# The second FFN's output pass in rows: activations held in TensorE, weights streamed, and the residual turned during the input pass

## Chip, cores and metric

One core of one Trainium2 chip. The metric is the device time of the program in microseconds (us); the kernel before takes 1973.4 us, the median of 3 runs (1972.02 to 1973.48).

## What is computed

One layer of a decoder on 1024 tokens of width 1024 in float32: an FFN of half weight, a mixing part (a gated recurrence and an attention, side by side), and a second FFN of half weight. Only the second FFN matters here:

```python
def swiglu(h, w_in, w_out):
    gu = h @ w_in
    g, u = jnp.split(gu, 2, axis=-1)
    return (jax.nn.silu(g) * u) @ w_out
...
        h = h + 0.5 * swiglu(rms_norm(h, ffn2_norm[l]), ffn2_w_in[l], ffn2_w_out[l])
    return h[:, pad + N_META:, :]
```

`w_in` is 1024 x 5632, `w_out` 2816 x 1024. The output is (1, 1024, 1024): tokens by features, so a row of the output is a token.

## The kernel before

Inside the kernel the residual h lies turned: `hT[:, m, t]` holds feature 128 m + p of token t on partition p. After the mixing part its turned form is also in DRAM, as `h2D` (8 blocks of 128 features x 1024 tokens), because the second FFN normalizes the copy on chip in place.

Both passes of the FFN use a fast (Strassen-Winograd) form of a 2 x 2 block product: seven block products in place of eight. Every float32 operand is split into a rounded part and the rest ("wh" and "wl" for a weight, "xh" and "xl" for an activation), and each product is three matmuls: wh by xh, wl by xh, wh by xl.

*Input pass* (`fast_in`, line 359). Columns of `w_in` are taken 128 at a time, in pairs f, f+1; a pair has two quads: the first (the "gate" quad, line 537) applies SiLU, the second (the "up" quad, line 546) multiplies. One quad loads four blocks of 128 x 4 x 128 from `w_in` (`block`, line 376, on SP's queue, each bound behind the one before), makes four sums of them on GpSimd (`made`, line 385), splits seven operands (`operand`, line 367: ScalarE rounds at L369, VectorE subtracts at L371), and runs seven products of 12 matmuls each (`times`, L458) into the banks qa, qb and qc, two buffers each. VectorE adds bank and kept parts (L490, L541, L548, L551, L552). The activations go to DRAM (`actD`) by GpSimd's queue, and some of their sums too (`combined`, line 562). The first four quads use weights split earlier; 18 quads follow that load from `w_in`.

*Output pass* (`fast_out`, line 624). `w_out` is taken as 2 x 2 blocks of 1408 x 512, and the activations as 2 x 2 blocks of 1408 features x 512 tokens. Seven steps (A12, A11, S1, S2, S4, S3, A22, line 709) each go over q = 0..10; a q loads a weight block and an activation block of 128 x 512 on SP's queue, splits both (`halved`, line 652, ScalarE L656 and VectorE L657, four places each in `parts`, so up to four q ahead), and runs 12 matmuls (L733): four blocks m of 128, three products each. The stationary operand is a 128 x 128 block of the weight, the moving one the activations of 512 tokens, so bank m gets 128 features x 512 tokens. Bank sets x and y are used in turn; x is started in A11 and added to in S2, S3 and A22, y is started in A12 and S1 and added to in S4. `evict` (line 700) adds half a bank to the residual on VectorE (L703): of A12, A11, S1, S2 and S4 in the next step, at q = 1 and q = 3; of S3 and A22 at once. The quadrants are final after A11, S4, S3 and A22.

The residual is loaded from `h2D` into `hT` on SP's queue during A12, A11 and S2 (line 2347). When the second half of the tokens is final (after S3) and when the first is (after A22), `store_out` (line 1058) turns it back: for four blocks of 128 tokens and two halves of the features, four TensorE transposes (L1065) into a bank, a copy by ScalarE (L1068) or VectorE (L1070), and a store of 256 KB on SP's queue (L1071).

TensorE runs in the order of the code; the other engines' orders come from a scheduler, which `issue_after` binds. An engine's queue runs in order, so a DMA that waits on SP holds all that is behind it.

The first FFN does a like turning of its input x during its own input pass (`turn_x`, line 1016): load, a VectorE transpose of 32 x 32 blocks (L1047), and four stores of 64 KB each in pieces of 32 elements (L1050).

Of the kernel before, what the change touches and what calls it, by code (L numbers as in the profile page):

```python
# [11 lines left out]
F32 = mybir.dt.float32  # L12
# [8 lines left out]
P = 128  # L21
# [28 lines left out]
class Block:  # L50
# [308 lines left out]
    def fast_in(self, ops, n, w_in, actD, openers, ev0, open_ev, feed=None, meta=None, spare=None,  # L359
# [7 lines left out]
        def operand(src):  # L367
            hi = wp.tile([P, 4, P], F32R, tag="wh", name="wh", bufs=3)
            nc.scalar.copy(hi, src)  # L369
            lo = wp.tile([P, 4, P], F32R, tag="wl", name="wl", bufs=3)  # L370
            nc.vector.tensor_sub(lo, src, hi.bitcast(F32))  # L371
            return hi, lo

        loaded, put_off, last_kept = [], [], []
# [1 line left out]
        def block(i, h, col):  # L376
            t = wp.tile([P, 4, P], F32, tag="raw", name="raw", bufs=self.in_bufs)
            with self.tc.issue_after(loaded[-1].ins) if loaded else ExitStack():
                loaded.append(nc.sync.dma_start(
                    t, w_in[512 * h : 512 * h + 512, col + P * i : col + P * i + P]  # L380
                    .rearrange("(k p) f -> p k f", p=P)
                ))
            return t

        def made(x, op, y, turns):
# [236 lines left out]
            put_off.pop()()  # L622

    def fast_out(self, hT, cs, n, w_out, actD, ready, between=lambda a, q: None,
                 meta=lambda a, q, blocks: None):

        nc = self.nc
        op, ring, pout = self.op, self.ring, self.pout
# [70 lines left out]

        def evict(bank, i, j, step, ms=range(4)):  # L700
            for m in ms:
                h = hT[:, 4 * i + m, cs[j] : cs[j] + n]
                nc.vector.scalar_tensor_tensor(  # L703
                    h, banks[bank][m], 0.5, h, ALU.mult, ALU.add
                )
            if 3 in ms:
                ready(step)

# [6 lines left out]
        for bank, a, b, start, (i, j) in steps:  # L715
            if start:
                banks[bank] = [
                    pout.tile([P, n], F32, tag=f"{bank}{m}", name="o") for m in range(4)
                ]
            for q in range(nq):  # L720
                with self.tc.issue_after(los[-4]) if self.apart and len(los) > 4 else ExitStack():
                    src, blocks = left(a, q)
                act = right((q, b), n)
                with self.tc.high_priority() if self.apart and a == "A12" and q < 3 else ExitStack():
                    wh, wl = halved(src, "w", 512)
                    xh, xl = halved(act, "t", n)
                order = [(m, e, q, wh, wl, xh, xl) for m in range(4) for e in range(3)]
                if a == "A12" and q < 3:
                    opening += order
                    order = sorted(opening, key=lambda o: (o[1], o[2])) if q == 2 else []  # L730
                for m, e, at, wh, wl, xh, xl in order:
                    y, z = ((wh, xh), (wl, xh), (wh, xl))[e]
                    nc.tensor.matmul(  # L733
                        banks[bank][m], y[:, m * P : (m + 1) * P], z,
                        start=start and at == 0 and e == 0,
                        stop=q == nq - 1 and e == 2, skip_group_check=True,
                    )
                meta(a, q, blocks)
                between(a, q)
                if q in (1, 3) and delayed:  # L740
                    evict(*delayed[0], range(q - 1, q + 1))
                    if q == 3:
                        delayed.pop()
            if a in ("S3", "A22"):
                evict(bank, i, j, a)
            else:
                delayed.append((bank, i, j, a))
# [307 lines left out]
                row = load(i + 1)  # L1055
            yield

    def store_out(self, hT, pool, pps, c0, n, tag):
        nc = self.nc
        for i, r0 in enumerate(range(c0, c0 + n, P)):  # L1060
            for q in range(2):
                row = pool.tile([P, 512], F32, tag="orow", name="orow", bufs=4)
                ps = pps.tile([P, 4, P], F32, tag=f"{tag}{(2 * i + q) % 4}", name="o")
                for k in range(4):
                    nc.tensor.transpose(ps[:, k, :], hT[:, 4 * q + k, r0 : r0 + P], self.ident)  # L1065
                dst = row.rearrange("p (k c) -> p k c", k=4)
                if q == 0:
                    nc.scalar.copy(dst, ps)  # L1068
                else:
                    nc.vector.tensor_copy(dst, ps)  # L1070
                nc.sync.dma_start(self.out[0, r0 : r0 + P, 512 * q : 512 * q + 512], row)  # L1071

    def proj_bank(self, n):
        self.proj_tags.reverse()
# [686 lines left out]
    def run(self):  # L1761
# [21 lines left out]
        with ExitStack() as c0:  # L1783
            with ExitStack() as c1:
# [373 lines left out]
                with tc.manual_schedule(engines={nc.tensor.engine}):  # L2158
# [38 lines left out]

                    self.weave(rest(), heads[:3], 1e6, 1.0, True)
            self.h2D = self.dram.tile([KT, P, SEQ], F32, name="h2D")
            ph = self.pool("h2")  # L2200
            hT = ph.tile([P, KT, SEQ], F32, tag="h2", name="hT2", bufs=1)
            (cA, n), (cB, _) = ((0, 512), (512, 512))
# [10 lines left out]
            with tc.manual_schedule(engines={nc.tensor.engine}), ExitStack() as cx:  # L2213
# [94 lines left out]
                rs = []  # L2308
                made = feed()
                def after_opened():  # L2310
                    both = ph.tile([P, 16, n], F32R, tag="h2", name="parts", bufs=1)
                    self.parts = {"w": both[:, :8], "t": both[:, 8:]}

                steps = self.fast_in(
                    ops, n, a["ffn2_w_in"][0], actD, 2, ev0, open_ev, made,
                    after_opened=after_opened,
                )
                next(steps)
                r = self.inv_rms_rows(sums[1], n, px, ppb)
# [6 lines left out]
                drain(steps)  # L2326
            with tc.manual_schedule(engines={nc.tensor.engine}), ExitStack() as c1:
                self.ring = self.pool("ring", ctx=c1, side="right")
                hT = self.pool("h3", ctx=c1).tile([P, KT, SEQ], F32, name="hT3")
                self.op = self.pool("op", ctx=c1)  # L2330
                self.pout = self.pool("pout2", 1, PSUM, c1)
                fin = self.pool("fin", ctx=c1)

                def ready(step):
                    if step == "S3":
                        self.store_out(hT, fin, self.pout, cB, n, "y")
                    elif step == "A22":
                        self.store_out(hT, fin, self.pout, cA, n, "y")

                loads = {("A12", 2 * m): (m, cA) for m in range(4)}  # L2340
                loads.update({("A11", m): ((m + 4) % 8, cB) for m in range(8)})
                loads.update({("S2", m): (m + 4, cA) for m in range(4)})

                def between(step, q):
                    if (step, q) in loads:
                        m, c = loads[step, q]
                        nc.sync.dma_start(hT[:, m, c : c + n], self.h2D[m, :, c : c + n])

                self.ring_bufs, self.act_bufs, self.apart = 6, 6, False
                self.fast_out(hT, (cA, cB), n, a["ffn2_w_out"][0], actD, ready, between)  # L2350


NAMES = [
# [21 lines left out]
```

## Time and profile before

| | |
|---|---|
| median of 3 runs | 1973.4 us |
| profiled execution | 1973.63 us |
| its span in the profile | 1971.9 us |
| granted clock of TensorE, mean | 0.999 |
| TensorE matmul busy | 1936.1 us (98%) |
| VectorE, ScalarE, GpSimd busy | 1390.4, 854.9, 445.0 us |
| output pass of the second FFN, start to last matmul | 1748.92 to 1962.36 us |

Positions are microseconds from the span's start. PE is TensorE's matmuls, PEld its weight loads (they overlap), DVE VectorE, ACT ScalarE, POOL GpSimd, SP SyncE; a q behind the name means the engine's queue, with its DMA issues and waits. A row of the timeline gives start, length, engine, line, operation, tile written <- tiles read, shapes, count, and in brackets the idle time of the engine before it and what ended it.

### The profile page before, as it was taken

To read this page: it belongs to the slowest core of one execution; us is meant where nothing else is said; L and a number is where in the kernel's file an instruction comes from. 1 tells how busy PE (TensorE), PEld (TensorE's weight loads), DVE (VectorE), ACT (ScalarE), POOL (GpSimd) and SP (SyncE) were. 2 spreads that over 40 slices of the span, in tenths; PEclk is the share of its full clock that TensorE was granted. 3 is DMA by queue.
4 is the path that set the end of the run, shared out by engine and by line. 5 is a ranking of instruction groups with operands and counts; after the bars stand their busy time and mean duration, and the time that the engine had idled before them with its cause. 6 is when DMAs were issued, how large, how long until landed. Compare 5 with 4: busy or idle time off the path is not lost.

```text
span 1971.9 us, 30437 instructions
## 1 busy us (share of the span) xinstructions
PE 1936.1 (98%) x10768; PEld 1629.3 (83%) x10768; DVE 1390.4 (71%) x2178; ACT 854.9 (43%) x1719; POOL 445.0 (23%) x614
## 2 busy tenths in 40 slices
PE   7999999999999999999999999999999999999998
PEld 6888888888888888888898978887888888888887
DVE  7977777877678665467777666667577766767764
ACT  6523343334444544366666635433223333344443
POOL 3010100001000003133333342210545544620000
PEclk9999999999999999999999999999999999999999
DMA  7356787758966325765454178646433323378463
GB/s 210 93 164 169 250 272 240 243 192 299 371 217 189 117 61 149 178 181 146 126 148 118 58 248 244 161 184 203 160 106 108 108 94 104 102 281 295 123 193 139
DMA packets 346362, 347.17 MB, mean 176 GB/s; under 512 B 94993, under 2 KB 250513, under 8 KB 346209
## 3 DMA queue, kind: packets, MB, share of 16 engines
q1 hardware_dynamic: 325360, 283.73, 47.1%
q0 software_dynamic: 19808, 61.49, 9.0%
q8 instruction: 85, 1.39, 0.3%
q14 instruction: 69, 0.56, 0.1%
q10 hardware_dynamic: 1040, 0.00, 0.0%
HBM read 233.75 MB, written 111.38 MB: 175 GB/s over the span
## 4 chain that ended last, share of the span: by engine, by line
PE 73%; issue 16%; DVE 4%; DMA 2%; POOL 2%; ACT 2%; SPq 1%; POOLq 0%; DVEq 0%; ACTq 0%
PE o L733 21%; PE qb L458 11%; PE qa L458 8%; PE qc L458 7%; PE proj L258 4%; PE proj L260 4%; PE proj L259 4%; PE flip L1479 2%; PE wo L259 1%; PE wo L258 1%; PE wo L260 1%; PE oacc L1554 1%; PE oacc L1556 1%; PE z L1624 1%; DMA KB<-hg_k 1%
## 5 line engine op out<-in xcount | busy, mean ns | idle before, releaser
L458 PE MATMUL qb<-T,wh 128*128 128x512 f32 x1056 | 344.4, 390 | 1.3 <-ACT T L318 0.8
L458 PEld LDWEIGHTS qb<-T,wh 128*128 128x128 f32 x1056 | 198.1, 188 | 46.1 <-issue 2.5
L458 PE MATMUL qa<-B,wh 128*128 128x512 f32 x696 | 226.8, 391 | 0.0
L258 PE MATMUL proj<-xh,wh 128*128 128x512 f32 (+2 forms) x640 | 213.4, 333 | 2.4 <-ACT st L1126 1.3
L733 PE MATMUL o<-t,w 128*128 128x512 f32 x924 | 212.2, 390 | 0.6 <-DVE u L551 0.5
L260 PE MATMUL proj<-xl,wh 128*128 128x512 f32 (+2 forms) x640 | 209.8, 328 | 0.8 <-DVE xl L1948 0.8
L733 PE MATMUL o<-parts 128*128 128x512 f32 x924 | 209.9, 389 | 0.0
L259 PE MATMUL proj<-xh,wl 128*128 128x512 f32 (+2 forms) x640 | 209.8, 328 | 0.0
L458 PE MATMUL qb<-T,wl 128*128 128x512 f32 x528 | 205.5, 389 | 0.0
L733 PEld LDWEIGHTS o<-t,w 128*128 128x128 f32 x924 | 172.7, 188 | 37.8 <-issue 0.8
L733 PEld LDWEIGHTS o<-parts 128*128 128x128 f32 x924 | 173.3, 188 | 36.0
L371 DVE TENSOR_TENSOR wl<-s,wh 128x512 fp32r<-128x512 f32 x160 | 165.7, 1035 | 50.8 <-ACT wh L369 49.8
L369 ACT CAST wh<-s 128x512 fp32r<-128x512 f32 x160 | 99.4, 622 | 194.1 <-PE qb L458 146.1
L458 PEld LDWEIGHTS qa<-B,wh 128*128 128x128 f32 x696 | 130.7, 188 | 27.3 <-DVE B L837 0.3
L369 ACT CAST wh<-raw 128x512 fp32r<-128x512 f32 x120 | 74.4, 621 | 148.0 <-PE qc L458 108.0
L458 PE MATMUL qa<-B,wl 128*128 128x512 f32 x348 | 135.6, 390 | 0.0
L258 PEld LDWEIGHTS proj<-xh,wh 128*128 128x128 f32 x640 | 120.6, 188 | 14.4 <-ACT st L1126 1.9
L260 PEld LDWEIGHTS proj<-xl,wh 128*128 128x128 f32 x640 | 120.4, 188 | 12.1 <-DVE xl L1948 1.2
L259 PEld LDWEIGHTS proj<-xh,wl 128*128 128x128 f32 x640 | 120.5, 188 | 9.9
L458 PE MATMUL qc<-T,wh 128*128 128x512 f32 x352 | 117.1, 394 | 0.0
L458 PE MATMUL qc<-B,wh 128*128 128x512 f32 x352 | 115.0, 390 | 1.4 <-DVE u L551 1.4
L458 PEld LDWEIGHTS qb<-T,wl 128*128 128x128 f32 x528 | 99.1, 188 | 20.3
(399 smaller groups left out, 3865.6 us busy)
## 6 DMA issues: line engine op xcount, KB each, us to landing
raw<-in_ffn_w_in_dram SPq DMA_DIRECT2D x176, 256.0 KB, 4.1
raw<-in_ffn_w_out_dram SPq DMA_DIRECT2D x112, 256.0 KB, 4.3
w2in<-both SPq DMA_DIRECT2D x28, 512.0 KB, 3.4
raw<-in_w_in_dram SPq DMA_DIRECT2D x25, 512.0 KB, 5.2
ks<-kD SPq DMA_DIRECT2D x32, 260.0 KB, 4.8
wout<-both SPq DMA_DIRECT2D x16, 512.0 KB, 3.8
wh<-w2in SPq DMA_DIRECT2D x27, 256.0 KB, 3.3
wl<-w2in SPq DMA_DIRECT2D x27, 256.0 KB, 3.2
```

Of the source, the lines that this page charges most:

```text
L258: nc.tensor.matmul(ps, wh[:, s], xs, start=k == 0, stop=False)
L259: nc.tensor.matmul(ps, wl[:, s], xs, start=False, stop=False)
L260: nc.tensor.matmul(ps, wh[:, s], xl[:, k, c0 : c0 + n], start=False, stop=k == nk - 1)
L369: nc.scalar.copy(hi, src)
L371: nc.vector.tensor_sub(lo, src, hi.bitcast(F32))
L458: nc.tensor.matmul(ps, a[:, k, :], b[:, k, :], start=start and k == 0 and i == 0, stop=k == 3 and i == 2, skip_group_check=True,)
L733: nc.tensor.matmul(banks[bank][m], y[:, m * P : (m + 1) * P], z, start=start and at == 0 and e == 0, stop=q == nq - 1 and e == 2, skip_gro ...
L1479: self.nc.tensor.transpose(ps[:m, j, :], src[:, s0 : s0 + m], self.ident)
L1554: nc.tensor.matmul(o[:, c], vj, w[0], start=j == 0, stop=False, skip_group_check=True)
L1556: nc.tensor.matmul(o[:64, c], vj[:, :64], w[1], start=False, stop=end, skip_group_check=True)
L1624: nc.tensor.matmul(z, q, ks[0][:, s0 : s0 + n], start=True, stop=False)
```

## The change

1. In the output pass of the second FFN the two operands of each matmul change places (`rows=True`): the stationary block is 128 tokens of the activation, the moving one 512 features of the weight. Bank m then holds 128 tokens x 512 features, and the residual tile is `hR`, with rows of tokens.
2. The final quadrants are stored from `hR` straight after their eviction, 128 tokens x 512 features at a time: those of A11, S4 and S3 on GpSimd's queue, those of A22 on SP's. `store_out`, its TensorE transposes and its copies are gone.
3. The residual must be there in rows. A new generator, `turn_back`, goes over 16 places (8 blocks of features x 2 halves of the tokens) during the input pass, a step after each of the 18 quads: it loads 128 x 512 of `h2D`, transposes 32 x 32 blocks on VectorE (bound behind the last "wl" of the quad), and stores it in four pieces into `h2R` in DRAM (bound behind the quad's last weight load). The output pass loads `hR` from `h2R`, in the places where it loaded `hT` from `h2D`.

```diff
@@ operand, block (fast_in)
-            nc.vector.tensor_sub(lo, src, hi.bitcast(F32))
+            self.block_lo = nc.vector.tensor_sub(lo, src, hi.bitcast(F32))
...
+            self.block_load = loaded[-1]
@@ evict (fast_out)
-                h = hT[:, 4 * i + m, cs[j] : cs[j] + n]
+                h = (hT[:, 4 * j + m, 512 * i : 512 * i + 512] if rows
+                     else hT[:, 4 * i + m, cs[j] : cs[j] + n])
                 nc.vector.scalar_tensor_tensor(
                     h, banks[bank][m], 0.5, h, ALU.mult, ALU.add
                 )
+                if rows and step in ("A11", "S4", "S3", "A22"):
+                    r0 = n * j + P * m
+                    eng = nc.sync if step == "A22" else nc.gpsimd
+                    eng.dma_start(self.out[0, r0 : r0 + P, 512 * i : 512 * i + 512], h)
...
                     y, z = ((wh, xh), (wl, xh), (wh, xl))[e]
+                    if rows:
+                        y, z = z, y
                     nc.tensor.matmul(
                         banks[bank][m], y[:, m * P : (m + 1) * P], z,
@@ store_out is replaced by
+    def turn_back(self, pool, src, dst):
+        nc, tc = self.nc, self.tc
+        places = [(m, half) for half in range(2) for m in range(KT)]
+        def load(i):
+            m, half = places[i]
+            t = pool.tile([P, 512], F32, tag="hcol", name="hcol", bufs=2)
+            with tc.issue_after(self.block_load.ins):
+                nc.sync.dma_start(t, src[m, :, 512 * half : 512 * half + 512])
+            return t
+        def store(t, m, half):
+            for b in range(4):
+                c0 = P * m + 32 * b
+                with tc.issue_after(self.block_load.ins):
+                    nc.sync.dma_start(
+                        dst[512 * half : 512 * half + 512, c0 : c0 + 32]
+                        .rearrange("(f j) d -> j f d", j=32),
+                        t[32 * b : 32 * b + 32].rearrange("j (f d) -> j f d", d=32),
+                    )
+        cols = load(0)
+        yield
+        for i, place in enumerate(places):
+            t = pool.tile([P, 512], F32, tag="hrow", name="hrow", bufs=2)
+            with tc.issue_after(self.block_lo.ins):
+                nc.vector.transpose(t, cols)
+            if i + 1 < len(places):
+                cols = load(i + 1)
+            yield
+            store(t, *place)
@@ run
+                    back.append(self.turn_back(self.pool("hturn", ctx=cx), self.h2D, h2R))
...
-                    after_opened=after_opened,
+                    after_opened=after_opened, between=turn_next,
...
-                hT = self.pool("h3", ctx=c1).tile([P, KT, SEQ], F32, name="hT3")
+                hR = self.pool("h3", ctx=c1).tile([P, SEQ // P, D], F32, name="hR")
...
-                        nc.sync.dma_start(hT[:, m, c : c + n], self.h2D[m, :, c : c + n])
+                        r, i = loads[step, q]
+                        nc.sync.dma_start(
+                            hR[:, r, 512 * i : 512 * i + 512],
+                            h2R[P * r : P * r + P, 512 * i : 512 * i + 512],
+                        )
```

How it moves instructions shows at three places. On TensorE, from the end of the input pass to the end of the program, before ("qc" is the input pass, "o<-parts" the output pass, "o<-ident" the transposes):

```order
L458 MATMUL qc<-B_14181,wl 128x512
L458 MATMUL qc<-B_14182,wh 128x512
L733 MATMUL o<-parts 128x512 x792
L1065 MATMUL o<-ident,hT_17639 128x128 x32
L733 MATMUL o<-parts 128x512 x132
L1065 MATMUL o<-ident,hT_17639 128x128 x32
```

and now:

```order
L459 MATMUL qc<-B_14183,wh 128x512
L459 MATMUL qc<-B_14182,wh 128x512
L459 MATMUL qc<-B_14182,wl 128x512
L459 MATMUL qc<-B_14183,wh 128x512
L741 MATMUL o<-parts 128x512 x924
```

The two runs of 32 transposes are gone, and the 924 matmuls of the output pass follow each other.

On VectorE, in a gate quad of the input pass, where its last operand is split, before ("wl" is the rest of a split weight, "sg" and "u" are sums of banks):

```order
L371 TENSOR_TENSOR wl<-raw,wh 128x512
L490 TENSOR_TENSOR u_15238<-qb,p_15177 128x512
L371 TENSOR_TENSOR wl<-s,wh 128x512
L541 TENSOR_TENSOR sg<-qc,u_15238 128x512
L371 TENSOR_TENSOR wl<-raw,wh 128x512
L541 TENSOR_TENSOR sg<-qb,p_15177 128x512
L371 TENSOR_TENSOR wl<-s,wh 128x512
```

and now:

```order
L371 TENSOR_TENSOR wl<-raw,wh 128x512
L491 TENSOR_TENSOR u_15248<-qb,p_15187 128x512
L371 TENSOR_TENSOR wl<-s,wh 128x512
L1092 STREAM_TRANSPOSE hrow<-hcol 128x512
L542 TENSOR_TENSOR sg<-qc,u_15248 128x512
L371 TENSOR_TENSOR wl<-raw,wh 128x512
L542 TENSOR_TENSOR sg<-qb,p_15187 128x512
L371 TENSOR_TENSOR wl<-s,wh 128x512
```

The transpose stands between the split of the quad's last operand and the sum of bank qc; in an up quad it stands in front of the sum of L551 in the same way.

On SP's queue, over the 18 quads, before (72 weight loads in one row, then the output pass begins):

```order
L402 DMA wl<-w2in_908 128x512
L402 DMA wh<-w2in_908 128x512
L379 DMA raw<-in_ffn_w_in_dram 128x4x128 x72
L642 DMA raw<-in_ffn_w_out_dram 128x512
L647 DMA act<-act0B_12583 128x512
```

and now, at the start of the 18 quads ("hcol" is the loaded piece, "hrow" the transposed one; the last three rows go on alike for the other places):

```order
L1074 DMA hcol<-h2D 128x512
L379 DMA raw<-in_ffn_w_in_dram 128x4x128 x4
L1074 DMA hcol<-h2D 128x512
L379 DMA raw<-in_ffn_w_in_dram 128x4x128 x7
L1081 DMA h2R<-hrow 32x16x32 x4
L1074 DMA hcol<-h2D 128x512
L379 DMA raw<-in_ffn_w_in_dram 128x4x128 x4
```

The four stores and the next load stand between the third and the fourth weight load of a quad; these loads run ahead of the operands, so the stored place was transposed two quads before the quad whose weights stand around it. The last stores stand right ahead of the output pass's first load.

More of the change, by code (lines that the diff above doesn't have):

```diff
@@ L624, in fast_out @@
     def fast_out(self, hT, cs, n, w_out, actD, ready, between=lambda a, q: None,
-                 meta=lambda a, q, blocks: None):
+                 meta=lambda a, q, blocks: None, rows=False):
         nc = self.nc
@@ L1056, in turn_x @@
             yield
[L1058 to L1071, printed above, removed]
+    def turn_back(self, pool, src, dst):
[26 more added lines that the diff above has]
+            store(t, *place)
     def proj_bank(self, n):
@@ L2199, in run @@
             self.h2D = self.dram.tile([KT, P, SEQ], F32, name="h2D")
+            h2R = self.dram.tile([SEQ, D], F32, name="h2R")
             ph = self.pool("h2")
```

22 lines of the change are left out of this document (11 added, 11 removed).

## The prediction

> **What bounds the kernel now.** I read the page first, then a table of busy time by stretch of the second FFN, the chain of work that ended last, and the timeline around the places that the diff touches.
>
> ```profile
> PE 1936.1 (98%) x10768; PEld 1629.3 (83%) x10768; DVE 1390.4 (71%) x2178; ACT 854.9 (43%) x1719; POOL 445.0 (23%) x614
> ```
>
> TensorE's matmuls (PE) fill 98% of the span. The table splits the end of the kernel; its columns are the stretch, its length, the busy time and count of PE, weight loads, VectorE, ScalarE and GpSimd, then the granted clock, the DMA share and GB/s:
>
> ```profile
> 1600.00:1638.00 38.00, 38.00 (x168) 31.20 (x167) 26.88 (x29) 12.06 (x20) 19.11 (x19) 1.00 0.32 104
> ...
> 1748.92:1928.29 179.37, 179.37 (x794) 148.44 (x792) 125.19 (x199) 74.59 (x131) 7.48 (x9) 1.00 0.69 231
> 1928.29:1932.14 3.85, 3.73 (x33) 3.37 (x32) 3.85 (x7) 2.32 (x5) 0.00 (x0) 1.00 0.40 140
> ...
> 1962.36:1971.90 9.54, 3.71 (x32) 3.24 (x30) 3.50 (x6) 2.34 (x4) 0.00 (x0) 0.88 0.57 221
> ```
>
> In the input pass (first row, two quads of it) and in the output pass PE never stops. So time can leave in two ways only: PE gets fewer instructions, or the end behind the last matmul gets shorter. It can come back in one way: PE is made to wait. The PE timeline shows both places of the first kind, the two runs of 32 transposes (L1065):
>
> ```profile
> 1928.29 4.10 PE L1065 MATMUL o<-ident,hT 128*128 128x128 f32 x32
> 1932.14 30.22 PE L733 MATMUL o<-parts 128*128 128x512 f32 x132
> 1962.20 3.90 PE L1065 MATMUL o<-ident,hT 128*128 128x128 f32 x32
> ```
>
> The chain that ended last runs through the first run of transposes, then straight through the last 132 matmuls, then through transpose, copy and store:
>
> ```profile
> 1929.29 0.04 issue
> 1929.33 3.05 PE o L1065 x25
> 1932.39 29.97 PE o L733 x132
> 1962.36 0.76 PE o L1065 x7
> ```
>
> **The change, part by part.** *1. Operands swapped (L733).* Each of the 924 matmuls still loads one 128x128 block and streams 512 columns; both kinds of operand are halves of "parts", with the same shape and type. Their rate does not change: 0 us. From both sides I take nothing lost or gained, since weight loads (148.44 of 179.37 us) stay beside PE.
>
> *2. The first 32 transposes go.* Step A22's matmuls now follow S3's at once, at 1928.29 instead of 1932.14: **3.85 us**. What could be late next is bank x, which A22 goes on adding to: it must have been read by the four evictions of S3.
>
> ```profile
> 1926.80 2.48 DVE L703 SCALAR_TENSOR_TENSOR hT<-o,hT 128x512 f32<-128x512 f32 x4
> ```
>
> They start 1926.80 and end 1929.28, one each 0.6 us. A22 needs bank m only 3 matmuls after bank m-1 (0.68 us at 30.22 / 132 = 0.229 us each): at 1928.3, 1929.0, 1929.7 and 1930.3, and the evictions end at about 1927.5, 1928.1, 1928.7 and 1929.3. Each is 0.8 to 1 us early, so the whole 3.85 us goes. If A22 waited for all four, 1.0 us would stay. ScalarE and VectorE prepare operands up to four q ahead, and lose 8 copies; nothing new there.
>
> *3. The tail.* Behind the last matmul (1962.36) stand four evictions, 32 transposes, eight copies and eight stores:
>
> ```profile
> 1960.35 2.74 DVE L703 SCALAR_TENSOR_TENSOR hT<-o,hT 128x512 f32<-128x512 f32 x4 [7.12 <-PE o L733]
> ...
> 1963.44 5.26 SPq L1071 DMA_DIRECT2D out_dram<-orow x8
> ```
> ```profile
> L1071 SPq DMA_DIRECT2D out_dram<-orow x16: 332/335/453, 1929.9 to 1968.4; - x16
> ...
> DMA to landing us min/median/max: 2.0/2.3/3.6
> ```
>
> The last store is issued at 1968.4 (1963.44 + 5.26 - 0.33). In the changed kernel it comes right behind the last eviction, which ends at 1960.35 + 2.74 = 1963.09; with the 0.04 us that the chain has between S3's evictions and what waits for them that is 1963.13. So **5.24 us** go. The four stores are as large as those before (256 KB), 0.7 us apart; I keep the 2.3 us of landing, and hold its maximum, 3.6 us, as the bad end (+1.3 us), its minimum as the good one (-0.3 us).
>
> *4. Twelve stores on GpSimd's queue.* They follow the evictions of A11 (during S1), S4 (during S3) and S3. GpSimd has nothing left to do in the last 140 us, and the queue holds nothing behind them. 1 MB more around 1812 meets a DMA share of 0.69 on average, but S1 is loaded by then; its last sum of raw blocks is this:
>
> ```profile
> 1809.01 0.69 DVE L671 TENSOR_TENSOR sk<-raw 128x512 f32<-128x512 f32 x1 [0.85 <-DMA raw<-in_ffn_w_out_dram]
> ```
>
> 0 us, by the room of operands that are made ahead; cover gone would mean a q's loads late by about 1 MB at the 231 GB/s of this stretch, 4.5 us.
>
> *5. The turning of the residual, 16 places in 18 quads of the input pass.* Each adds a 256 KB load and four 64 KB stores on SP and a 32x32-block transpose on VectorE. The first FFN does the same to x, in rows of this trace:
>
> ```profile
> L1047 DVE STREAM_TRANSPOSE xts<-xrow x16: 701/704/712, 112.5 to 352.5; 128x512 f32<-128x512 f32 x16
> ...
> L1050 SPq DMA_DIRECT2D xD<-xts x64: 303/586/1784, 113.2 to 356.9; - x64
> ...
> DMA to landing us min/median/max: 1.8/3.8/5.9
> ```
>
> VectorE: in the "up" quads the transpose falls into 1.32 us of idleness. In the "gate" quads VectorE is full up to 1612:
>
> ```profile
> 1590.24 0.69 DVE L551 TENSOR_TENSOR u<-qc,u 128x512 f32<-128x512 f32 x1 [1.32 <-PE qc L458]
> ...
> 1599.53 3.44 DVE L371 TENSOR_TENSOR wl<-s,wh 128x512 fp32r<-128x512 f32 x1 [1.91 <-ACT wh L369]
> 1602.90 0.68 DVE L490 TENSOR_TENSOR u<-qb,p 128x512 f32<-128x512 f32 x1
> ...
> 1608.88 1.18 DVE L371 TENSOR_TENSOR wl<-s,wh 128x512 fp32r<-128x512 f32 x1
> 1609.98 0.68 DVE L541 TENSOR_TENSOR sg<-qc,u 128x512 f32<-128x512 f32 x1
> 1610.58 1.39 DVE L371 TENSOR_TENSOR wl<-raw,wh 128x512 fp32r<-128x512 f32 x1
> 1612.23 0.69 DVE L541 TENSOR_TENSOR sg<-qb,p 128x512 f32<-128x512 f32 x1 [0.25 <-PE qb L458]
> ...
> 1614.95 0.69 DVE L541 TENSOR_TENSOR sg<-qc,u 128x512 f32<-128x512 f32 x1 [1.30 <-PE qc L458]
> ```
> ```profile
> 1614.91 2.72 PE qa L458 x12
> ...
> 1633.95 2.72 PE qa L458 x12
> ```
>
> (The last two rows are the starts of two quads on PE, 19.0 us apart.) The transpose goes between 1608.88's and 1609.98's instruction, and queues everything behind it by 0.7 us; the idle 0.25 and 1.30 us give that back by 1615. Who waits for the delayed ones: the "wl" that ends at 1611.97 is read by the second matmul of the block at 1614.91, at 1615.14, so 3.17 us are free. The same operation there takes 0.69 to 3.44 us while GpSimd computes, and no row shows a transpose beside GpSimd. So its price lies between 0.70 us (L1047) and 3.44 us. I take 0.70: "u", which reads one operand from PSUM, stands at 0.68 between stretched neighbours, and the transpose also reads one operand from SBUF. With 3.44, 3.44 - 3.17 = 0.27 us are lost in each of 8 gate quads: 2.2 us.
>
> The Trainium skill, page "SBUF — State Buffer", section "Who interferes with whom", says that a VectorE instruction with two SBUF inputs shares a read port with GpSimd and is held, one with at most one SBUF input outside the two-port modes is not. The rows of "wl" and "u" agree. By it the sum has 0 for the 2.2 us.
>
> SP: the four stores stand ahead of the quad's last weight load, behind a transpose that has ended.
>
> ```profile
> 1608.38 3.44 SPq L379 DMA_DIRECT2D raw<-in_ffn_w_in_dram  x2
> 1612.00 0.37 SPq L379 DMA_DIRECT2D raw<-in_ffn_w_in_dram  x1
> 1620.89 0.37 SPq L379 DMA_DIRECT2D raw<-in_ffn_w_in_dram  x1
> ```
> ```profile
> raw<-in_ffn_w_in_dram SPq DMA_DIRECT2D x176, 256.0 KB, 4.1
> ```
> ```profile
> 1633.99 0.62 ACT L369 CAST wh<-raw 128x512 fp32r<-128x512 f32 x1 [2.05 <-PE qc L458]
> ```
>
> The stores go in at 1611.8, and the load of 1612.00 (the block that ScalarE rounds at 1633.99) is put off by 4 x 0.59 + 0.59 = 2.9 us. It has 22 us, of which 4.1 us (the median of such loads) are landing. The next load, 1620.89, is untouched. DMA: 512 KB per quad of 19.0 us are 28 GB/s on a share of 0.32. 0 us. The last stores go out behind the transpose of the 17th quad, six quads behind the one at 1610, so near 1725; with 2.3 us of issue and 5.9 of landing they are done by about 1734. The first load of rows is due where now "hT" is:
>
> ```profile
> 1745.70 2.03 SPq L2347 DMA_DIRECT2D hT<-h2D  x3
> ```
>
> **Sum.** 3.85 + 5.24 = 9.09 us. The profiled execution took 1973.63 us (span 1971.9), so 1964.5; the median of the three runs, 1973.4, is 0.2 us lower: 1964.3. I take **1964.4 us**.
>
> **Rivals.** *A, part of the gain stays away* (0.12): the stretched transpose (2.2 us) and the slow landing (1.3 us) give 1964.4 + 3.5 = 1967.9; A22 waiting for all of S3's evictions gives 1965.4. For it: no row bounds the transpose beside GpSimd. Against: free time of 3.17 us. *B, slower* (0.07): the weight load behind the four stores comes late and PE waits in the input pass. It decides when stores and hcol hold that load over 18 us (22 - 4.1); at 1 us over in 16 quads it is 1964.4 + 16 = 1980.4. For it: 512 rows of 128 bytes per store, 3.8 us for 64 KB where the plain store of 256 KB takes 2.3 us; four in series and a load as large as a weight block are 4 x 3.8 + 4.1, which is 19.3 us, a whole quad. Against: in the first FFN these stores ran beside more traffic and PE stayed full:
>
> ```profile
> 280.00:310.00 30.00, 30.00 (x191) 25.01 (x190) 22.65 (x38) 12.38 (x23) 3.71 (x7) 1.00 0.88 273
> ```
>
> The Trainium skill, page "DMA: Bandwidth & Descriptors", section "Specifications", puts full rate at 512 bytes and more, with a read-modify-write below. The landings agree in direction; this is rival B's rule, and by it alone the time would be B's, 1980.4. *C, the change does not do what it says* (0.05): the turning is not hidden by the input pass, the rows in DRAM are not ready when asked for at 1745.7, SP's queue stands with the output pass's weights behind it, and the wait eats the gain. It has 11 us (1745.7 - 1734); 20 us late gives 1964.4 + 9 = 1973.4.
>
> **How the numbers follow.** Forecast 0.76, A 0.12, B 0.07, C 0.05. A difference of 0.2% (3.9 us) is about what can be told from none. Faster: 0.76 + 0.12 = 0.88; same: 0.05; slower: 0.07. The range goes up to A's 1967.9, so 1968, and down by the landing's 0.3 us and the spread of the runs before (1972.02 against 1973.4, 1.4 us) to 1962.7; outside it lie B and C.
>
> **What would show it.** After: PE without transposes in the second output pass and without idleness between S3 and A22; the last store issued about 0.8 us behind the last matmul; 16 block transposes at 0.70 us; PE 38.00 of 38.00 in the input pass. A gap of PE before a block whose "wl" is late speaks for A, one before a block whose weights were still landing for B, SP standing before the first load of rows for C. A gain from matmuls at another pitch than 0.229 us would prove step 1 wrong.

## The result, and the profile after

| | before | after |
|---|---|---|
| median | 1973.44 us (1971.98 to 1975.29, 6 runs) | 1964.75 us (1963.01 to 1965.29, 6 runs) |
| profiled execution | 1973.63 us | 1965.29 us |
| its span | 1971.9 us | 1963.6 us |

After takes 0.9954 of the time of before (95% interval 0.9941 to 0.9967): 8.7 us less, where 9.1 were forecast.

The page of after, its row of busy time (share of the span, count of instructions):

```profile
PE 1928.3 (98%) x10704; PEld 1622.0 (83%) x10704; DVE 1391.6 (71%) x2186; ACT 851.7 (43%) x1711; POOL 449.8 (23%) x626
```

64 TensorE instructions and 7.8 us of its busy time are gone. VectorE has 8 instructions more: 16 block transposes come, its share of the 16 copies goes. GpSimd has 12 more, the stores.

The same two stretches that the prediction showed of before (length, then busy time and count of PE, weight loads, VectorE, ScalarE, GpSimd; clock; DMA share; GB/s):

```profile
1600.00:1638.00 38.00, 38.00 (x168) 31.17 (x167) 27.83 (x30) 11.74 (x21) 19.08 (x20) 1.00 0.45 129
1748.92:1928.29 179.37, 179.37 (x793) 148.50 (x793) 125.28 (x199) 74.77 (x130) 12.62 (x17) 1.00 0.72 244
```

PE is still full in both. The input pass now moves 129 GB/s in place of 104, the 25 more against 28 forecast, and the DMA share went from 0.32 to 0.45. The output pass keeps its pitch: 793 matmuls in 179.37 us, 794 before (the stretch is the same in both, and after starts its output pass 1.1 us into it).

The timeline at the end of after, by engine (start, length, what; in brackets the idle time before it), and the chain of work that ended last:

```profile
1914.66 44.81 PE L741 MATMUL o<-parts 128*128 128x512 f32 x197
```
```profile
1928.89 2.34 POOL L711 DMA_DIRECT2D out_dram<-hR  x4 [25.42 <-DVE hR L705]
```
```profile
1958.20 2.37 SPq L711 DMA_DIRECT2D out_dram<-hR  x4
```
```profile
1914.83 42.63 PE o L741 x188
1957.45 0.02 issue
1957.48 2.73 DVE hR L705 x4
```

PE runs as one row through the place where step A22 follows S3 (132 matmuls before its end, about 1929.5) up to 1959.47; S3's stores go out on GpSimd's queue beside it. Behind the last matmul only the evictions' end (1957.48 + 2.73 = 1960.21) and the last store are left, issued at 1960.2 (1958.20 + 2.37 is its end).

To place the gain, the starts of the two passes of the second FFN in both kernels, from the chain. The first fence is before, the second after:

```profile
1404.34 2.72 PE qa L458 x12
...
1748.92 16.09 PE o L733 x71
```
```profile
1405.41 2.72 PE qa L459 x12
...
1750.04 15.19 PE o L741 x67
```

From the first quad that loads its weights to the output pass it is 344.58 us before (1748.92 - 1404.34), 344.63 after (1750.04 - 1405.41). From there to the last matmul it was 213.44 us (1962.36 - 1748.92), now 209.43: 4.01 less. From the last matmul to the end of the span it was 9.54 us, now 4.13: 5.41 less. That is 9.4 us. The span is only 8.3 us shorter, because this execution of after reached the quad at 1404.34 already 1.07 us later, ahead of all that the change touches; it is the slowest of its six runs.

### The profile page after: what moved, and what is told of

The parts are those of the page before. It is cut to its first block, busy times and chain, and to the rows that moved or that the text cites. A ratio compares the mean times of both kernels' runs of the same rounds, so it can differ in the third digit from the quotient of the medians.

```text
span 1963.6 us, 30437 instructions
## 1 busy us (share of the span) xinstructions
PE 1928.3 (98%) x10704; PEld 1622.0 (83%) x10704; DVE 1391.6 (71%) x2186; ACT 851.7 (43%) x1711; POOL 449.8 (23%) x626
## 4 chain that ended last, share of the span: by engine, by line
PE 91%; DVE 4%; DMA 2%; ACT 2%; issue 1%; POOL 0%; SPq 0%; ACTq 0%; DVEq 0%; POOLq 0%
PE o L741 21%; PE qb L459 18%; PE qc L459 12%; PE qa L459 12%; PE proj L258 5%; PE proj L260 5%; PE proj L259 5%; PE flip L1504 2%; PE wo L259 1%; PE wo L260 1%; PE wo L258 1%; PE mq L1010 1%; PE oacc L1579 1%; PE oacc L1581 1%; PE z L1649 1%
## 5 line engine op out<-in xcount | busy, mean ns | idle before, releaser
L371 DVE TENSOR_TENSOR wl<-s,wh 128x512 fp32r<-128x512 f32 x160 | 165.8, 1036 | 50.8 <-ACT wh L369 49.8
```

Of the source, the lines that this page charges most:

```text
L371: self.block_lo = nc.vector.tensor_sub(lo, src, hi.bitcast(F32))
```

## The experiments

Ratios are to the kernel before on the same chip. Its medians there were 1974.13 us (beside *mid_plain*, *end_plain*, *out_turned*, *no_turn*), 1972.81 (*t8*, *unbound*, *sp_stores*, *stores4*), 1974.12 (*early1*, *late4*) and 1972.61 (*pieces4*, *sums_late*). Twelve kernels ran.

### The gain in its two parts: mid_plain, end_plain, out_turned

*mid_plain* is the kernel before, but after S3 it stores its second half of the tokens as it lies in `hT`, in eight plain stores on GpSimd's queue. A quarter of the output is written twice, and a quarter not at all.

```diff
+def plain(ks, c0, eng):
+    for k in ks:
+        eng.dma_start(self.out[0, P * k : P * k + P, c0 : c0 + n], hT[:, k, c0 : c0 + n])
...
 if step == "S3":
-    self.store_out(hT, fin, self.pout, cB, n, "y")
+    plain(range(8), cB, nc.gpsimd)
```

> The kernel before with only the first of its two turnings back taken out: after S3 the second half of the tokens is stored as it lies, eight stores on GpSimd's queue (that half of the output comes out turned). My theory: PE loses 32 transposes and nothing waits underneath, so 3.9 us less, ratio 0.998. Rival (A22 has to wait for S3's evictions, which the transposes had covered): 2.9 us or less, and a gap on PE between S3 and A22.

Measured: 1970.37 us, 0.9977 (0.9967 to 0.9986), so 3.8 us less, where 3.9 were expected.

*end_plain* does the same at the end alone: four plain stores after A11, four after A22; again a quarter twice and a quarter not.

```diff
+if step == "A11":
+    plain(range(4), cA, nc.gpsimd)
 elif step == "A22":
-    self.store_out(hT, fin, self.pout, cA, n, "y")
+    plain(range(4, 8), cA, nc.sync)
```

> The kernel before with only the second turning back taken out: the first half of the tokens is stored as it lies, four stores after A11 on GpSimd's queue and four after A22 on SP's (that half comes out turned). My theory: the tail behind the last matmul falls from 9.5 to 4.1 to 4.3 us, so 5.2 to 5.4 us less, ratio 0.9973; the first 32 transposes stay at 3.85 us of PE. Rival (the final stores of 256 KB queue up behind each other and land late): 4 us less.

Measured: 1968.24 us, 0.9968 (0.9956 to 0.9981), so 5.9 us less; 5.2 to 5.4 were expected, and the interval holds them. Its chain has the first run of transposes still, and the short end:

```profile
1929.16 3.06 PE o L1065 x25
1932.22 27.91 PE o L733 x123
1960.13 0.02 issue
1960.16 2.73 DVE hT L703 x4
```

From the start of the last evictions to the end of the span it is 1966.3 - 1960.16 = 6.1 us. It was 1971.9 - 1960.35 = 11.6 us before, and is 1963.6 - 1957.48 = 6.1 us after. Against before, the end is worth 5.4 us in both profiles.

*out_turned* does both at once, every quadrant stored as it lies, operands as before, no turning: the output is the transposed one.

```diff
+at = {"A11": (0, cA), "S4": (0, cB), "S3": (4, cB), "A22": (4, cA)}
+if step in at:
+    k, c0 = at[step]
+    plain(range(k, k + 4), c0, nc.sync if step == "A22" else nc.gpsimd)
```

> The kernel before with its operands as they were, but the four final quadrants of the turned residual are stored as they lie, each after its last addition (those of A11, S4 and S3 on GpSimd's queue, those of A22 on SP's): no TensorE transposes, no copies, no turning of the residual. It leaves out the turning of the result, which comes out features by tokens. My theory (the gain is 3.85 us of mid transposes and 5.2 us of tail, and the turning in the input pass costs nothing): as the changed kernel, 8.5 to 9.5 us under the kernel before, ratio 0.9952 to 0.9957. Rival (the turning costs its transposes on VectorE, 16 x 0.7 us): about 20 us under, ratio 0.990.

Measured: 1964.33 us, 0.9947 (0.9935 to 0.9960). That is 9.8 us less, a little over the 8.5 to 9.5 expected; the two parts give 3.8 + 5.9 = 9.7. So the whole gain is there without the swapped operands and without the turning. *no_turn*, below, has the swap and no turning: 1964.11 us beside 1964.33 on the same chip, so the swap costs nothing that can be told.

### What the turning costs: no_turn, t8

*no_turn* is after without the turning; `hR` is loaded from `h2D`, so the residual added is a misplaced one.

```diff
-    back.append(self.turn_back(self.pool("hturn", ctx=cx), self.h2D, h2R))
...
-        h2R[P * r : P * r + P, 512 * i : 512 * i + 512],
+        self.h2D[r, :, 512 * i : 512 * i + 512],
```

> The changed kernel without the turning: the 16 loads, transposes and 64 stores are gone, and the output pass loads its rows from the turned residual in DRAM, by loads of the same size (the residual added is therefore in the wrong places). My theory (the turning is wholly hidden): within 1 us of the changed kernel, ratio 0.995 to 0.996 against the kernel before. Rival (it costs some of VectorE's time or the weights' loads): 2 to 11 us under the changed kernel, ratio 0.990 to 0.9945.

Measured: 1964.11 us, 0.9947 (0.9935 to 0.9960), beside 0.9954 (0.9941 to 0.9967) of after: the intervals are almost the same. By them alone the turning could still cost 2 us or so; the trace is sharper, with the input pass at 344.63 us in after and 344.58 before, and no wait of PE in it. The 16 loads, 16 transposes and 64 stores are hidden.

*t8* does each block transpose eight times.

```diff
-    nc.vector.transpose(t, cols)
+    for _ in range(8):
+        nc.vector.transpose(t, cols)
```

> The changed kernel with every block transpose of the turning done eight times over (same tiles): 112 more VectorE instructions of 0.6 to 0.7 us. My theory of the free time (3.17 us in a gate quad before the split a11 block is late, and a quad of 19.0 us on which VectorE is busy for 13.3 to 15.5 us): eight of them, 5.0 us, go past it by about 1.8 us in each of 8 gate quads, so PE waits for VectorE and the kernel is 10 to 25 us slower than the changed one. Rival (VectorE's delay is taken up by the places of the operands made ahead): under 2 us.

Measured: 1983.94 us, 1.0046 (1.0031 to 1.0061), about 19 us more than after. PE's waits from 1400 on (total, times, longest), then VectorE ahead of one of them:

```profile
PE qa L459 <- DVE wl L371: 18.9, 8, 2.4
```
```profile
1598.40 2.20 DVE L1093 STREAM_TRANSPOSE hrow<-hcol 128x512 f32<-128x512 f32 x3
...
1605.86 0.70 DVE L1093 STREAM_TRANSPOSE hrow<-hcol 128x512 f32<-128x512 f32 x1
...
1607.05 0.69 DVE L371 TENSOR_TENSOR wl<-raw,wh 128x512 fp32r<-128x512 f32 x1
```

All eight waits are of one kind: the first block of a gate quad waits 2.36 us or so for its "wl" (L371, 1607.05), which stands behind the eight transposes of the up quad ahead of it. Seven more are 7 x 0.70 = 4.9 us; 2.4 are lost, so 2.5 us were still free there. Behind the gate quads, where the prediction had placed the danger, PE never waited: there the scheduler put only four of the eight transposes ahead of the next quad's first "wl" (at 1623.49, for a block that PE starts at 1626.73). So the size came as expected and the place did not, and the 3.17 us that the prediction had worked out for the gate quads were not put to the test.

### Where it is put: unbound, sp_stores

*unbound* is after without the three bindings of `turn_back` (load and stores behind the quad's last weight load, transpose behind its last "wl").

```diff
-    with tc.issue_after(self.block_load.ins):
         nc.sync.dma_start(t, src[m, :, 512 * half : 512 * half + 512])
...
-    with tc.issue_after(self.block_load.ins):
         nc.sync.dma_start(dst[...], t[...])
...
-    with tc.issue_after(self.block_lo.ins):
         nc.vector.transpose(t, cols)
```

> The changed kernel without the three bindings of the turning (behind the weight loads and behind the split of the last operand): the scheduler then puts the first seven places into the opening of the input pass, stores ahead of the prepared weights, and transposes anywhere. My theory: the bound order is what keeps the price at nothing; unbound, stores that wait for a transpose stand ahead of weights on SP's queue and PE waits in the opening quads, 2 to 15 us slower than the changed kernel. Rival (there is room enough anywhere): within 1 us.

Measured: 1973.13 us, 0.9996 (0.9987 to 1.0006): the whole gain is gone. The stretches before 1500 of *unbound*, and behind them those of after:

```profile
1300.00:1400.00 100.00, 95.55 (x427) 78.00 (x426) 71.15 (x125) 31.32 (x57) 14.81 (x22) 0.98 0.67 200
1400.00:1500.00 100.00, 97.72 (x430) 80.14 (x429) 71.03 (x78) 29.77 (x50) 53.05 (x52) 1.00 0.57 154
```
```profile
1300.00:1400.00 100.00, 98.66 (x448) 81.27 (x448) 67.35 (x118) 32.30 (x59) 15.41 (x23) 1.00 0.49 168
1400.00:1500.00 100.00, 100.00 (x440) 82.25 (x440) 73.99 (x77) 31.92 (x53) 56.65 (x54) 1.00 0.44 136
```

PE loses 3.1 and 2.3 us to idleness there, and 2 hundredths of clock over 100 us; that is about the 7.5 us by which the two spans differ. From 1500 on it is full. VectorE and PE at the first of the two waits, just ahead of the input pass (L1698 adds a product of the mixing part to the residual):

```profile
1301.10 0.71 DVE L1092 STREAM_TRANSPOSE hrow<-hcol 128x512 f32<-128x512 f32 x1 [4.44 <-DMA hcol<-h2D]
...
1303.74 0.68 DVE L1698 TENSOR_TENSOR hT<-wo,hT 128x512 f32<-128x512 f32 x1
```
```profile
1304.47 0.50 PE L258 MATMUL wo<-oH,wh 128*128 128x512 f32 x1 [3.10 <-DVE hT L1698]
```

VectorE stood 4.44 us in front of a transpose whose load had not landed, and the addition that PE needed stood behind it. The second wait, 2.28 us at 1428.91, is alike: a sum of L542 (1428.12) stands right behind a transpose (1427.48) in front of which VectorE had stood idle for 3.17 us. So the loss is of the size expected and not of the kind: stores did hold SP's queue for their transposes (four times, up to 16.6 us), but PE waited for no weights. The transposes are free where they are bound, and not anywhere.

*sp_stores* moves the twelve stores from GpSimd's queue to SP's.

```diff
-    eng = nc.sync if step == "A22" else nc.gpsimd
+    eng = nc.sync
```

> The changed kernel with the twelve stores that go on GpSimd's queue moved to SP's queue, where loads of weights and activations stand behind them. My theory: a store there waits for its eviction while the loads behind it stand, but operands are made up to four q ahead and blocks loaded six ahead, so within 1 us of the changed kernel; the choice of the queue is then without effect. Rival: the loads come late and PE waits, 2 us or more slower.

Measured: 1963.94 us, 0.9946 (0.9930 to 0.9962). The choice of queue makes no difference that can be told, as expected.

### Rival B, and two theories that fell: stores4, early1, late4, pieces4, sums_late

*stores4* does every store of the turning four times, three of them into spare DRAM.

```diff
-    for b in range(4):
+    for dst, b in [(x, b) for x in (*spare, src_rows) for b in range(4)]:
```

> The changed kernel with every one of the 64 stores of the turning done four times, three of them into other rows of DRAM: 192 more stores of 64 KB in pieces of 128 bytes. My theory: SP's fourth weight load of a quad is put off by about 10 us, of 18 us that are free, and the DMA share of the input pass rises from 0.45 to about 0.8, so the time stays within 1 us of the changed kernel. Rival (the small pieces hold the DMA engines, and weights come late): 15 us or more slower, with PE waiting for loads.

Measured: 2097.24 us, 1.0621 (1.0605 to 1.0637), 132 us more than after, where 1 us at most was expected. My theory of an ample cover seemed to fall by this run (the later runs show that more had changed in it than the stores). On SP the stores also stood three weight loads earlier than in after (from the second place on behind load 16, 20, 24 and so on of the pass, in place of 19, 23, 27). So the next theory was that the place costs, not the number.

*early1* puts the stores of after, once each, at that earlier place.

```diff
+    self.stored = nc.sync.dma_start(dst[...], ...)
...
 with self.tc.issue_after(loaded[-1].ins) if loaded else ExitStack(), \
+        self.tc.issue_after(self.stored.ins) if getattr(self, "stored", None) else ExitStack():
     loaded.append(nc.sync.dma_start(
```

> The 64 stores once each, as in the kernel after, but with each quad's first weight load bound behind the stores of the quad before, so that on SP's queue they stand ahead of the first load of a quad in place of ahead of its last: three loads earlier, where the run with fourfold stores had them. Theory (the place on SP's queue makes the loss: the store waits there for its transpose and holds the weight loads behind it): 70 to 140 us slower than after, that is 2035 to 2105 us. Rival (the number of small pieces makes the loss): within 3 us of after, 1964 to 1968 us.

Measured: 1964.13 us, 0.9950 (0.9934 to 0.9967): as after. The place theory fell too. SP's waits in this kernel from 1400 to 1750, and its timeline:

```profile
SPq L1082 <- DVE hrow L1093: 228.1, 16, 16.9
```
```profile
1610.16 1.97 SPq L1082 DMA_DIRECT2D h2R<-hrow  x4
...
1612.77 2.04 SPq L380 DMA_DIRECT2D raw<-in_ffn_w_in_dram  x4
1627.30 1.97 SPq L1082 DMA_DIRECT2D h2R<-hrow  x4
```

In each of 16 quads the stores hold SP's queue for 14.3 us on average, up to 16.9, with all four weight loads of a quad behind them, and PE does not wait once from 1400 on.

*late4* has the fourfold stores a quad later, behind transposes long done.

```diff
-    t = pool.tile([P, 512], F32, tag="hrow", name="hrow", bufs=2)
+    t = pool.tile([P, 512], F32, tag="hrow", name="hrow", bufs=3)
...
-    store(t, *place)
+    if i:
+        store(*kept)
+    kept = t, *place
+store(*kept)
```

> Every store four times as in the run with fourfold stores, but a quad later (three buffers for the transposed tile), so that on SP's queue they stand one load behind where they stand in the kernel after, and their transpose is long done. Theory (the place makes the loss): 0 to 25 us slower than after, 1964 to 1990 us: 16 issues of 0.59 us are 9.4 us ahead of a weight load with 18 us free, and some us may go at the start of the output pass, ahead of whose loads 32 stores stand. Rival (the small pieces load the queue or the DMA engines): 100 to 140 us slower than after, 2065 to 2105 us.

Measured: 2073.48 us, 1.0502 (1.0487 to 1.0518), 109 us more than after: the rival's size. So neither place nor waiting transposes explain it. What PE waits for in *late4* led on: mostly for ScalarE's "wh", and ScalarE for a sum of GpSimd. GpSimd's timeline and ScalarE's at one such wait:

```profile
1582.26 1.28 POOL L571 TENSOR_TENSOR t<-sg,t 128x512 f32<-128x512 f32 x1
...
1584.40 1.27 POOL L391 TENSOR_TENSOR s<-raw 128x512 f32<-128x512 f32 x1
1585.75 1.26 POOL L391 TENSOR_TENSOR s<-s,raw 128x512 f32<-128x512 f32 x1
```
```profile
1587.05 0.62 ACT L369 CAST wh<-s 128x512 fp32r<-128x512 f32 x1 [17.18 <-POOL s L391]
```
```profile
1587.72 0.79 PE L459 MATMUL qb<-T,wh 128*128 128x512 f32 x1 [7.17 <-ACT wh L369]
```

The first sums of a gate quad's weights (L391) stand on GpSimd behind the sums of the activations of the pair before (L571), which can't start until PE has finished that pair. In after three of a gate quad's four stand ahead of them:

```profile
1585.73 1.30 POOL L391 TENSOR_TENSOR s<-s,raw 128x512 f32<-128x512 f32 x1 [0.68 <-POOL s L391]
...
1590.14 1.28 POOL L391 TENSOR_TENSOR s<-raw 128x512 f32<-128x512 f32 x1 [2.62 <-DVE wl L371]
...
1598.85 1.29 POOL L571 TENSOR_TENSOR t<-sg 128x512 f32<-128x512 f32 x1 [1.91 <-DVE sg L553]
```

The scheduler, given more stores, had ordered GpSimd's work otherwise, in *stores4* ahead of its last seven pairs and in *late4* ahead of its last six; in *early1* that order is the one of after.

ScalarE's order had changed too. *late4* at the start of an up quad, then after at the same place:

```profile
1552.03 0.63 ACT L543 ACTIVATE sg<-sg 128x512 f32<-128x512 f32 x1 [2.09 <-DVE sg L542]
1552.57 0.60 ACT L369 CAST wh<-raw 128x512 fp32r<-128x512 f32 x1
```
```profile
1553.22 0.49 PE L459 MATMUL qa<-B,wh 128*128 128x512 f32 x1 [1.95 <-ACT wh L369]
```
```profile
1610.68 0.62 ACT L369 CAST wh<-raw 128x512 fp32r<-128x512 f32 x1 [2.10 <-PE qc L459]
1612.43 0.63 ACT L543 ACTIVATE sg<-sg 128x512 f32<-128x512 f32 x1 [1.13 <-DVE sg L542]
```

In *late4* the up quad's first split stands behind the last SiLU of the gate quad, in after ahead of all three. With the "wl" that VectorE makes late in the same way, PE's waits at qa come to 28.0 us in *stores4* and 23.9 us in *late4*, 4.0 us a pair in both. Two last runs separate GpSimd's order from the pieces.

*pieces4* stores each transposed tile three more times, whole, in the same pieces of 32 elements: four times the pieces and bytes, but 7 DMAs a place and not 16, and the spare pieces land side by side in DRAM, not 4 KB apart as in `h2R`. The orders of the other engines stay those of after.

```diff
+    for _ in range(3):
+        with tc.issue_after(self.block_load.ins):
+            nc.sync.dma_start(
+                spare.rearrange("f p d -> p f d"), t.rearrange("p (f d) -> p f d", d=32)
+            )
     for b in range(4):
```

> The kernel after, with three more stores of each transposed tile into spare DRAM, each of the whole 128x512 tile in pieces of 32 elements: four times the pieces and bytes of the turning's stores, in 7 DMAs per place in place of 16. On SP they stand where the stores of after stand, and the orders of TensorE, VectorE, ScalarE and GpSimd are those of after word for word. Theory (in the two slow runs with fourfold stores the loss came from GpSimd's order of work, which the scheduler chose otherwise there: the sums of the next pair's weights behind the sums of the activations): 0 to 6 us slower than after, 1964 to 1971 us. Rival (the small pieces load the DMA engines or the queue): 60 to 140 us slower, 2025 to 2105 us.

Measured: 1964.01 us, 0.9956 (0.9940 to 0.9973): as after. A stretch of its input pass:

```profile
1600.00:1700.00 100.00, 100.00 (x440) 82.06 (x439) 68.37 (x77) 32.40 (x54) 55.28 (x51) 1.00 0.73 171
```

The DMA share is 0.73, and PE full.

*sums_late* stores once, and binds GpSimd's sums of weights behind the last sum of activations of the pair before.

```diff
-    taken(op(t, x, y), False)
+    with self.tc.issue_after(last_t[-1].ins) if last_t else ExitStack():
+        at = op(t, x, y)
+    taken(at, False)
...
-    sub(t, x, y)
+    at = sub(t, x, y)
+    if not meta:
+        last_t.append(at)
```

> The kernel after, stores once each, with one thing bound: GpSimd's sums of a pair's weights stand behind the last sum of the activations of the pair before, as the scheduler had them from the fifth pair on in the slow runs; here from the second pair on. Theory (that order makes the loss): the run with late fourfold stores lost 109 us over six pairs, 18 us a pair; over nine pairs 160 us, so 2070 to 2140 us. Rival (the number of stores makes the loss and the order does nothing): 1964 to 1970 us.

Measured: 2080.11 us, 1.0543 (1.0527 to 1.0559), 115 us more than after. PE's waits, one stretch, and one of the waits on three engines:

```profile
PE qb L461 <- ACT wh L369: 85.3, 9, 9.5
```
```profile
1600.00:1700.00 100.00, 80.40 (x327) 64.67 (x326) 39.94 (x59) 23.49 (x39) 37.46 (x38) 0.86 0.34 97
```
```profile
1565.61 1.28 POOL L573 TENSOR_TENSOR t<-sg,t 128x512 f32<-128x512 f32 x1
1566.83 1.27 POOL L392 TENSOR_TENSOR s<-raw 128x512 f32<-128x512 f32 x1
```
```profile
1569.92 0.62 ACT L369 CAST wh<-s 128x512 fp32r<-128x512 f32 x1 [8.18 <-POOL s L392]
```
```profile
1570.59 0.79 PE L461 MATMUL qb<-T,wh 128*128 128x512 f32 x1 [9.47 <-ACT wh L369]
```

One wait of 9.5 us in each of nine pairs, 85 us. The rest is clock: 0.86 was granted in this stretch, and a matmul took 80.40 / 327 = 0.246 us in place of 0.227; over the 168 of a pair that is 3.2 us, 29 us in nine. Together 114 of the 115 us. So the order of GpSimd's sums, without one more store, makes a large loss. That the total comes close to *stores4* and *late4* is chance: here it is nine pairs at 12.8 us (the expectation had 18), there seven at 19 us and six at 18 us. Their traces show what more there is in a pair: PE's wait for the late sums is 7.7 and 7.3 us there, the waits at qa are 4.0 us, which *sums_late* doesn't have, and the clock takes some 6 us (0.85 to 0.90 from 1500 on). From 1500 on neither run shows an engine waiting for a weight block of the input pass, but for one wait of VectorE in *late4* that ends with a DMA of SP's queue (2.5 us); so the weights were not late. At the start of the output pass, whose loads stand behind the last fourfold stores, PE waits 4.2 and 3.5 us more. No run has the waits at qa alone, and why the scheduler chose these orders stays open. In *sums_late* some instructions of ScalarE, VectorE and SP moved along with the sums.

## Why the prediction was right

*Step 1, operands swapped, 0 us.* Held: 793 matmuls in 179.37 us against 794, and *out_turned*, without the swap, has the time of *no_turn* and of after.

*Step 2, the first 32 transposes, 3.85 us.* 4.01 us in the trace, 3.8 in *mid_plain*. A22 does not wait for S3's evictions: PE has no gap there. Rival A's 1.0 us did not come.

*Step 3, the tail, 5.24 us.* 5.41 us in the trace, 5.9 in *end_plain* with an interval of 3.8 to 8.7. The end of the span lies 3.0 us behind the end of the last issue (1960.57), and lay 3.2 us behind it (1968.70) before: an end as long as before's, as was taken, and not the 1.3 us more of a late landing. That wasn't sure: the sixteen stores of after land 2.0 to 6.3 us behind their issue (median 4.0), past the 3.6 us that was held as the bad end, but the last one, issued at 1960.2, had at most 3.4 us.

*Step 4, twelve stores on GpSimd's queue, 0 us.* Held, and their place on that queue is no part of it (*sp_stores*).

*Step 5, the turning, 0 us.* Held (*no_turn*), and for the reasons given. The rows of it in after:

```profile
L1092 DVE STREAM_TRANSPOSE hrow<-hcol x16: 698/706/709, 1436.7 to 1726.1; 128x512 f32<-128x512 f32 x16
```
```profile
L1081 SPq DMA_DIRECT2D h2R<-hrow x64: 303/484/1498, 1438.6 to 1728.3; - x64
...
DMA to landing us min/median/max: 1.9/2.9/4.2
```
```profile
1610.02 1.18 DVE L371 TENSOR_TENSOR wl<-s,wh 128x512 fp32r<-128x512 f32 x1
1611.12 0.70 DVE L1092 STREAM_TRANSPOSE hrow<-hcol 128x512 f32<-128x512 f32 x1
1611.75 0.65 DVE L542 TENSOR_TENSOR sg<-qc,u 128x512 f32<-128x512 f32 x1
```

The transpose stands in the gate quad where it was put, between the "wl" of 1.18 us and the next "sg", and takes 0.70 us there as everywhere (698 to 709 ns), so the bound of 3.44 us can be dropped. The Trainium skill, page "SBUF — State Buffer", section "Who interferes with whom", had it that way: one read from SBUF is not held by GpSimd, two are; the trace agrees (0.70 beside 1.18 us). A store takes 0.48 us to issue, where 0.59 was taken, and lands in 2.9 us, where 3.8 was seen in the first FFN. The last stores begin at 1728.3, and with the longest issue and landing (1.5 and 4.2 us) they are down by 1734, as forecast. The loads of rows begin 12.7 us later:

```profile
L2374 SPq DMA_DIRECT2D hR<-h2R x16: 319/430/536, 1746.7 to 1809.2; - x16
```

*Rival B* did not come. Its condition, a weight load held over 18 us, was approached and not reached; two parts of it are apart now: small pieces, at four times the number, cost nothing (*pieces4*), and a queue held 14.3 us a quad, 16.9 at most, costs nothing (*early1*), which lies just inside the 18 us that the prediction had worked out from one load. The rule that stood behind rival B, in the Trainium skill, page "DMA: Bandwidth & Descriptors", section "Specifications" (full rate at 512 bytes and more), decides nothing here: pieces of 128 bytes at a DMA share of 0.73 left PE full.

*Rival C* did not come either. What the prediction did not see is what *unbound* showed: the turning is hidden by its bindings as much as by the room there is. Without them the gain is gone, around the start of the input pass and not at its end, and by way of VectorE: it stands in front of a transpose, and what PE needs stands behind it.

## What to carry to other kernels

Work at the end of a kernel that only reorders data is worth looking for twice: the layout can often be had from the matmul's choice of stationary operand, and what must be turned for it can be moved under a stage whose engine is full for other reasons, if it is bound to places where its inputs are there and nothing urgent stands behind it on its engine. When a run changes a number of instructions and the time jumps, compare the order of every engine first: the scheduler may have moved other work, and the jump may be that. A queue that waits is no loss by itself; follow the wait to the engine that sets the end.

## What was not expected of the hardware

While PE waited once per pair, its granted clock fell as well: 0.86 in the stretches of *sums_late*, 1.00 in after, and a matmul of 512 columns took 0.246 us in place of 0.227. A quarter of the loss of that run (29 of 115 us) is that clock and not the waiting.
